# Gate products of a hybrid S5 / stick-breaking layer: 16 pairs of units by Strassen's scheme, and a later load of z

## Chip, cores and metric

One core of one Trainium2 chip runs the whole layer in one launch. The metric is device time in microseconds, lower is better. The engines are named as in the profile: PE (matmul), PEld (its weight load), DVE (vector), ACT (scalar), POOL, SP (issues most DMAs).

## Reference

```python
h = concat([meta, x])                       # 16 + 512 rows, D_MODEL = 2048
u, g_ssm, q, k, v, g_sb = split(h @ w_in)
y_ssm = (s5_branch(u, ...) * silu(g_ssm)) @ w_branch_ssm
y_sb  = (stick_breaking_attention(q, k, v) * silu(g_sb)) @ w_branch_sb
gates = sigmoid(h @ w_gate + b_gate)        # 2048 -> 4096
mixed = gates[:, :2048] * y_ssm + gates[:, 2048:] * y_sb
out   = layer_norm(ALPHA * h + mixed @ w_out)[16:]
```

Everything is float32. `s5_branch` ends in a GLU whose input is called z below.

## The kernel before

**Products.** Each float32 product is made of three fp32r matmuls: both operands are split into a rounded part (hi) and the rest (lo), and `mm3` (L131) adds hi·hi, hi·lo and lo·hi into the same PSUM tile. X is held split in SBUF (`Xh`, `Xl`: 16 chunks of 128 channels by 512 real columns and the meta columns).

**Weights.** All weights lie in `wst` as chunks of 128 x 1024 in the order of use. SP loads a chunk into one of three `raw` buffers (`load_upto`, L112); `prep_upto` (L119) makes `whi` with an ACT cast (L126) and `wlo` with a DVE subtraction (`split_lo`, printed as L96, as is every `tensor_tensor`). `whi` and `wlo` have three buffers each.

**Order.** The program is written out by hand. A `slot` (L164) is the work of one chunk: eight pieces, a piece being three matmuls, or more where it has several outputs. At its start a slot records the preparation of the chunk two slots ahead, and the finish of the unit that ended before; at its sixth piece it records the load of the chunk five ahead. ACT, DVE and SP each take their instructions in the recorded order. `schedule` hangs other work (`fillers`) onto piece numbers.

**Stages around the change.** First come the projections of each head with the SSM and the attention between them, in matmuls of 256 and 272 columns or of 512. Then eight units for g_ssm (`fin_gs`): a unit is 128 output channels, 16 pieces, 48 matmuls of 512 columns. In the last three of these units `load_z` (L1071) brings z back from DRAM in eight parts: SP loads a part into the only `zt` buffer, ACT casts it into `zh`, DVE subtracts into `zl`. Then the gates: 32 units of the same form, `fin_gate` (L1096) being a sigmoid with bias of 128 x 512 and a store. Then the GLU (`unit_act` on `zh`, `zl`; its first unit reads all eight parts of z in its eight pieces), the branch products with the mixing, the output product and the layer norm.

Of the kernel before, what the change touches and what calls it, by code (L numbers as in the profile page):

```python
# [38 lines left out]
def kernel(  # L39
# [20 lines left out]
    V, A, PE, SP, G = nc.vector, nc.scalar, nc.tensor, nc.sync, nc.gpsimd  # L60

    def pool(name, bufs=1, space=None, side=None):
        kw = dict(name=name, bufs=bufs)
        if space is not None:
            kw["space"] = space
        else:
            kw["reuse_waits"] = "tile"
            if side is not None:
                kw["side"] = side
        st = ExitStack()  # L70
        p = st.enter_context(tc.tile_pool(**kw))
        return p, st
# [9 lines left out]
    raw_p = ctx.enter_context(tc.tile_pool(name="raw", bufs=3))  # L82
# [24 lines left out]
    raws, his, los = {}, {}, {}  # L107
    issued = [0]
    prepped = [0]
    held = {}  # L110

    def load_upto(c):  # L112
        while issued[0] <= min(c, NCH - 1):
            t = raw_p.tile([P, 1024], F32, tag="raw", name="raw")
            SP.dma_start(out=t, in_=wst[use[issued[0]]])
            raws[issued[0]] = t
            issued[0] += 1

    def prep_upto(c):  # L119
        while prepped[0] <= min(c, NCH - 1):  # L120
# [10 lines left out]
    def mm3(o, ah, al, bh, bl, start, stop):  # L131
        PE.matmul(o, ah, bh, start=start, stop=False)  # L132
        PE.matmul(o, ah, bl, start=False, stop=False)  # L133
        PE.matmul(o, al, bh, start=False, stop=stop)  # L134
# [9 lines left out]
    gtd = [dram.tile([P, S], F32, name=f"gtd{i}") for i in range(2 * KT)]  # L144
# [19 lines left out]
    def slot(pieces, finish=None, chunks=1, ahead=2):  # L164
        c = ctr[0]
        prep_upto(c + chunks - 1 + ahead)
        while pend:
            pend.pop(0)()
        h = [his.pop(c + x) for x in range(chunks)]
        lo = [los.pop(c + x) for x in range(chunks)]  # L170
        if chunks == 1:
            h, lo = h[0], lo[0]
        for k, f in enumerate(pieces):
            if k == 5 and ahead:
                load_upto(c + chunks - 1 + ahead + 3)
            run_fillers()
            f(h, lo)
            piece[0] += 1
        ctr[0] += chunks
        if finish is not None:  # L180
            pend.append(finish)

    with tc.manual_schedule():

        xp, x_st = pool("x", side="left")
        Xh = xp.tile([P, KT, LP], F32R, name="Xh")
        Xl = xp.tile([P, KT, LP], F32R, name="Xl")
# [67 lines left out]
        bga = const.tile([P, 32], F32, name="bga")  # L255
# [318 lines left out]
        def store_pv():  # L574
            for src, dst in pvt_:
# [3 lines left out]
                                            in_=zer[:, None, :].to_broadcast([16, NG, 112]))  # L579
# [23 lines left out]
        def ta(nm, shape, dt_=F32, bufs=1):  # L603
            return ma.tile(shape, dt_, tag=nm, bufs=bufs, name=nm)
# [337 lines left out]
        def new_acc():  # L942
            return acc_p.tile([P, 512], F32, name="acc")
# [61 lines left out]
        for i in range(NT):  # L1005
# [47 lines left out]
            if i == 0:  # L1053
                mb_st, at = open_main()
# [6 lines left out]


        def fin_gs(a, j):
            t = zst["p"].tile([P, S], F32, tag="gsg", bufs=2, name="gsg") if zst else ta("us", [P, L])[:, 0:S]
            A.activation(t, a, ACTF.Sigmoid)
            tt(t, a, t, ALU.mult)
            A.dma_start(out=gd[j], in_=t)

        zst = {}

        def load_z(j):  # L1071
            if not zst:
                mb_st.close()
                ma_st.close()
                c_st.close()
                zst["so"], zst["so_st"] = pool("so", side="right")
                zst["p"], zst["st"] = pool("z", side="right")
                zst["h"] = zst["p"].tile([P, NT, S], F32R, name="zh")
                zst["l"] = zst["p"].tile([P, NT, S], F32R, name="zl")
# [6 lines left out]
        for j in range(NT):  # L1086
            unit_real(lambda a, j=j: fin_gs(a, j))
        run_fillers()
        assert not fillers
        zh, zl = zst["h"], zst["l"]  # L1090
        sh_ = zst["so"].tile([P, NT, S], F32R, name="sh")
        sl_ = zst["so"].tile([P, NT, S], F32R, name="sl")
        tmpl = lambda nm, b=1: zst["p"].tile([P, S], F32, tag=nm, bufs=b, name=nm)


        def fin_gate(a, j):  # L1096
            t = tmpl("gsg", 2)
            A.activation(t, a, ACTF.Sigmoid, bias=bga[:, j:j + 1])
            A.dma_start(out=gtd[j], in_=t)
# [6 lines left out]
        mp_, mhl_st = pool("mhl", side="left")  # L1106
        ctx.callback(mhl_st.close)
        mh = mp_.tile([P, KT, S], F32R, name="mh")
        ml = mp_.tile([P, KT, S], F32R, name="ml")
        ohp, oh_st = pool("oh", side="left")  # L1110
        oh_ = ohp.tile([P, NT, S], F32R, name="oh")
        ol_ = ohp.tile([P, NT, S], F32R, name="ol")
# [69 lines left out]
        pend.pop(0)()  # L1182
        ct_st.close()
        oh_st.close()
        zst["so_st"].close()
# [6 lines left out]
        for c in range(NCH - HOLD, NCH):  # L1192
# [4 lines left out]
        bias = fp.tile([P, D], F32, name="bias")  # L1197
# [73 lines left out]
        prep_upto(NCH - 1)  # L1271
# [114 lines left out]
```

## Time and profile before

| | |
|---|---|
| device time, three runs | 1471.38, 1472.03, 1474.52 us (median 1472.03) |
| profiled execution | 1473.17 us, its span 1471.4 us |
| PE busy | 1449.2 us, 7888 matmuls |
| DVE, ACT busy | 759.5 us, 409.9 us |
| mean granted TensorE clock | 0.995 |

The span runs from the first to the last instruction of the core. Matmuls overlap, so a matmul's own duration is longer than the distance from its start to the next one's; the distance is what it costs. The same holds in part for ACT and DVE, whose next instruction may start a little before the last one ends.

### The profile page before, as it was taken

To read this page: it belongs to the slowest core of one execution; us is meant where nothing else is said; L and a number is where in the kernel's file an instruction comes from. 1 tells how busy PE (TensorE), PEld (TensorE's weight loads), DVE (VectorE), ACT (ScalarE), POOL (GpSimd) and SP (SyncE) were. 2 spreads that over 40 slices of the span, in tenths; PEclk is the share of its full clock that TensorE was granted. 3 is DMA by queue.
4 is the path that set the end of the run, shared out by engine and by line. 5 is a ranking of instruction groups with operands and counts; after the bars stand their busy time and mean duration, and the time that the engine had idled before them with its cause. 6 is when DMAs were issued, how large, how long until landed. Compare 5 with 4: busy or idle time off the path is not lost.

```text
span 1471.4 us, 19233 instructions
## 1 busy us (share of the span) xinstructions
PE 1449.2 (98%) x7888; PEld 1257.1 (85%) x7888; DVE 759.5 (52%) x1145; ACT 409.9 (28%) x640; POOL 48.9 (3%) x95
## 2 busy tenths in 40 slices
PE   8999999999999999999999999999999999999996
PEld 7888999999999998888888888888888888888885
DVE  7987766666767667733222222222444444423357
ACT  5332323232323232323222222222332222221220
POOL 0840000000000000000000000000000000000000
PEclk9999999999999999999999999999999999999998
DMA  7354352525253434435333333333544444374223
GB/s 253 113 141 120 105 132 96 144 81 145 88 140 98 141 94 131 119 118 174 129 116 119 123 122 123 114 121 128 165 132 163 143 144 146 134 206 158 90 96 115
DMA packets 94040, 191.99 MB, mean 130 GB/s; under 512 B 28160, under 2 KB 41728, under 8 KB 93184
## 3 DMA queue, kind: packets, MB, share of 16 engines
q1 hardware_dynamic: 75248, 172.87, 38.8%
q10 hardware_dynamic: 18704, 17.90, 3.6%
q8 instruction: 62, 1.02, 0.3%
q14 instruction: 26, 0.21, 0.0%
HBM read 168.45 MB, written 22.28 MB: 130 GB/s over the span
## 4 chain that ended last, share of the span: by engine, by line
PE 95%; DVE 4%; DMA 0%; issue 0%; ACT 0%; SPq 0%; DVEq 0%; ACTq 0%
PE acc L132 27%; PE acc L133 27%; PE acc L134 27%; PE aux L132 3%; PE aux L134 2%; PE aux L133 2%; PE aux L771 1%; PE aux L732 1%; PE aux L767 1%; PE aux L878 1%; DVE Xl L96 1%; DVE wlo L96 1%; DMA xt<-xT 0%; PE aux L703 0%; PE aux L851 0%; PE aux L852 0%
## 5 line engine op out<-in xcount | busy, mean ns | idle before, releaser
L96 DVE TENSOR_TENSOR wlo<-raw,whi 128x1024 fp32r<-128x1024 f32 (+1 forms) x242 | 295.1, 1220 | 588.0 <-ACT whi L126 584.4
L132 PE MATMUL acc<-Xh,whi 128*128 128x512 f32 (+2 forms) x1664 | 576.4, 346 | 5.3 <-ACT whi L230 4.7
L133 PE MATMUL acc<-Xl,whi 128*128 128x512 f32 (+2 forms) x1664 | 570.3, 343 | 1.6 <-DVE Xl L96 1.2
L134 PE MATMUL acc<-Xh,wlo 128*128 128x512 f32 (+2 forms) x1664 | 569.1, 342 | 0.0
L126 ACT CAST whi<-raw 128x1024 fp32r<-128x1024 f32 x238 | 250.2, 1053 | 686.7 <-PE acc L133 570.1
L132 PEld LDWEIGHTS acc<-Xh,whi 128*128 128x128 f32 x1664 | 315.4, 190 | 40.7 <-ACT whi L230 4.7
L133 PEld LDWEIGHTS acc<-Xl,whi 128*128 128x128 f32 x1664 | 315.0, 189 | 36.5 <-DVE Xl L96 2.7
L134 PEld LDWEIGHTS acc<-Xh,wlo 128*128 128x128 f32 x1664 | 314.7, 189 | 35.5
L133 PE MATMUL acc<-sl,whi 128*128 128x512 f32 x128 | 49.8, 389 | 0.0
L134 PE MATMUL acc<-oh,wlo 128*128 128x512 f32 x128 | 49.8, 389 | 0.0
L132 PE MATMUL acc<-whi,mh 128*128 128x512 f32 x128 | 49.8, 389 | 0.0
L133 PE MATMUL acc<-wlo,mh 128*128 128x512 f32 x128 | 49.8, 389 | 0.0
L132 PE MATMUL acc<-zh,whi 128*128 128x512 f32 x128 | 49.8, 389 | 0.0
L133 PE MATMUL aux<-wlo,mh 128*128 128x512 f32 x128 | 49.8, 389 | 0.0
L134 PE MATMUL acc<-zh,wlo 128*128 128x512 f32 x128 | 49.8, 389 | 0.0
L132 PE MATMUL acc<-sh,whi 128*128 128x512 f32 x128 | 49.8, 389 | 0.0
L133 PE MATMUL acc<-ol,whi 128*128 128x512 f32 x128 | 49.8, 389 | 0.0
L132 PE MATMUL aux<-whi,mh 128*128 128x512 f32 x128 | 49.8, 389 | 0.0
L133 PE MATMUL acc<-zl,whi 128*128 128x512 f32 x128 | 49.8, 389 | 0.0
L134 PE MATMUL acc<-sh,wlo 128*128 128x512 f32 x128 | 49.8, 389 | 0.0
L132 PE MATMUL acc<-oh,whi 128*128 128x512 f32 x128 | 49.8, 389 | 0.0
L134 PE MATMUL aux<-whi,ml 128*128 128x512 f32 x128 | 49.8, 389 | 0.0
(233 smaller groups left out, 1474.2 us busy)
## 6 DMA issues: line engine op xcount, KB each, us to landing
raw<-wst SPq DMA_DIRECT2D x238, 512.0 KB
gtd<-gsg ACTq DMA_DIRECT2D x32, 256.0 KB
gt<-gtd SPq DMA_DIRECT2D x32, 256.0 KB
X<-brep SPq DMA_DIRECT2D x8, 512.0 KB
X<-pvd SPq DMA_DIRECT2D x16, 256.0 KB
X<-sd SPq DMA_DIRECT2D x8, 512.0 KB
xs<-xr SPq DMA_DIRECT2D x8, 512.0 KB
xt<-xT SPq DMA_DIRECT2D x7, 528.0 KB
```

Of the source, the lines that this page charges most:

```text
L96: eng.tensor_tensor(out, a, b, op)
L126: A.copy(h, t)
L132: PE.matmul(o, ah, bh, start=start, stop=False)
L133: PE.matmul(o, ah, bl, start=False, stop=False)
L134: PE.matmul(o, al, bh, start=False, stop=stop)
L732: PE.matmul(vp[:, g, 0:NK], W["vt"][:, g].rearrange("p r q -> p (r q)"), ut[:, g * NK:g * NK + NK], start=True, stop=True,)
L767: PE.matmul(yp[:, g, 0:SK], W["ot"][:, g].rearrange("p t c -> p (t c)"), hs[:, g * NK + MK - 1:g * NK + MK - 1 + SK], start=True, stop=False,)
L771: PE.matmul(yp[:, g, 0:SK], W["mt"][:, g, :], ut[:, g * NK + MK:g * NK + MK + SK], start=False, stop=True,)
L878: PE.transpose(o, W["A"][:, k0:k0 + kn], ident)
```

## The change

The 32 gate units become 16 pairs. A pair is one 256-channel-wide block of the two gate halves (output channels j and 16+j), with X halved in two ways: by input channels (chunks 0 to 7 and 8 to 15) and by columns (0 to 255 and 256 to 511). Strassen's scheme (in Winograd's form) makes the four output quarters out of seven products instead of eight; each product is a slot of 24 matmuls of 256 columns. For that:

- `factor` makes four sums of weight chunks per pair on DVE, each 128 x 1024 (`s1`, `s2`, and two in place), so that the seven factors that are cast and split come from four loaded chunks. The fourth chunk has buffers of its own (`r22`).
- `sums_b` makes sums of X on DVE during the last g_ssm units, from X loaded a second time (`load_b`, 16 DMAs), splits three of them into `T1`, `T2`, `T3`, and leaves the fourth for `split_t4` in the first pair. These tiles take the place in SBUF that z had.
- `e0` to `e6` put the quarters together: one copy by ACT, five DVE sums of 256 columns, four sigmoids of 256 columns and two stores per pair. With `soon` they are recorded ahead of the preparation in a slot.
- z gets its tiles when the last pair has done with T1 to T3, and is loaded in that pair's last three slots (`open_z`, `load_z` every third piece). `zt` still has one buffer.
- The pools of the GLU and mixing stages change sides.

```diff
+    def factor(w, x):
+        if x == 0:
+            return w["11"]
+        if x == 1:
+            w["s1"] = sev["p"].tile([P, 1024], F32, tag="s1", name="s1")
+            w["s2"] = sev["p"].tile([P, 1024], F32, tag="s2", name="s2")
+            tt(w["s1"], w["21"], w["22"], ALU.add)
+            tt(w["s2"], w["s1"], w["11"], ALU.subtract)
+            return w["s2"]
+        if x == 2:
+            return w["s1"]
+        if x == 3:
+            tt(w["21"], w["11"], w["21"], ALU.subtract)
+            return w["21"]
+        if x == 4:
+            return w["12"]
+        if x == 5:
+            tt(w["s2"], w["12"], w["s2"], ALU.subtract)
+            return w["s2"]
+        return w["22"]
...
-            t = raws.pop(i)
+            pr = pair_of(i)
+            t = raws.pop(i) if pr is None else factor(sev[pr[0]], pr[1])
...
-    def slot(pieces, finish=None, chunks=1, ahead=2):
+    def slot(pieces, finish=None, chunks=1, ahead=2, soon=False):
         c = ctr[0]
+        while pend and soon:
+            pend.pop(0)()
         prep_upto(c + chunks - 1 + ahead)
...
+        def load_b(c):
+            t = sevst["xp"].tile([P, 2, L], F32, tag="xb", bufs=2, name="xb")
+            for e in range(2):
+                SP.dma_start(out=t[:, e, :], in_=xT[:, c + 8 * e, :])
...
+        def sums_b(c):
...
+            tt(b11, b12, b11, ALU.subtract)
+            tt(b12, b22, b12, ALU.subtract)
+            A.copy(row("1h"), b11)
+            tt(b22, b22, b11, ALU.subtract)
+            A.copy(row("3h"), b12)
+            tt(jk(sevst["t4"][:, c, :], SK), b21, b22, ALU.subtract)
+            A.copy(row("2h"), b22)
+            for x, b_ in (("1", b11), ("3", b12), ("2", b22)):
+                split_lo(row(x + "l"), b_, row(x + "h"))
+        schedule([(80, open_sev), (80, lambda: load_b(0)), (81, lambda: load_b(1))]
+                 + [(86 + 5 * c, lambda c=c: sums_b(c)) for c in range(8)]
+                 + [(87 + 5 * c, lambda c=c: load_b(c + 2)) for c in range(6)])
...
-        schedule([(80 + 6 * j, lambda j=j: load_z(j)) for j in range(NT)])
...
+        def pair(j):
+            tw = lambda nm, n=256: sev["p"].tile([P, n], F32, tag=nm, bufs=2, name=nm)
+            a, b, c = (new_acc()[:, 0:256] for _ in range(3))
+            ops = [
+                (a, Xh[:, 0:8, 0:256], Xl[:, 0:8, 0:256], True),
+                (b, sevst["2h"], sevst["2l"], True),
+                (c, sevst["1h"], sevst["1l"], True),
+                (b, sevst["3h"], sevst["3l"], False),
+                (a, Xh[:, 8:16, 0:256], Xl[:, 8:16, 0:256], False),
+                (c, Xh[:, 8:16, 256:512], Xl[:, 8:16, 256:512], False),
+                (b, t4h, t4l, False),
+            ]
...
+            def e3():
+                W[1] = tw("gb", S)
+                t = tw("u3")
+                tt(t, b, W["p1"], ALU.add)
+                tt(t, t, c, ALU.add)
+                sig(1, 1, t)
...
+            def e5():
+                tt(W["u2"], W["u2"], c, ALU.add)
+                sig(0, 1, W["u2"])
+                A.dma_start(out=gtd[j], in_=W[0])
+            def e6():
+                tt(W["p1"], W["p1"], b, ALU.add)
+                sig(1, 0, W["p1"])
+                A.dma_start(out=gtd[KT + j], in_=W[1])
...
+                if j == KT - 1 and x == 4:
+                    schedule([(0, open_z)] + [(1 + 3 * k, lambda k=k: load_z(k)) for k in range(NT)])
+                slot([mk(kk) for kk in range(8)], (e0, e1, None, e3, e4, e5, e6)[x], soon=True)
+        schedule([(4 + 6 * k, lambda k=k: split_t4(2 * k)) for k in range(4)])
+        for j in range(KT):
+            pair(j)
...
-        for j in range(KT):
-            unit_real(lambda a, j=j: fin_gate(a, j))
-            unit_real(lambda a, j=j: fin_gate(a, KT + j))
```

The order of the instructions at three places follows. In the changed kernel `raw` is a loaded chunk, `s_` a sum of chunks, `u_` and `p_` the sums of quarters.

DVE in the gates, before: one row, the split of each chunk.

```order
L96 TENSOR_TENSOR wlo<-raw,whi 128x1024 x65
```

DVE in one pair of the change, from the sum of `e5` of the pair before on:

```order
L96 TENSOR_TENSOR u_7316<-u_7316,acc 128x256
L96 TENSOR_TENSOR s_7449<-raw 128x1024
L96 TENSOR_TENSOR s_7450<-s_7449,raw 128x1024
L96 TENSOR_TENSOR wlo<-s_7450,whi 128x1024
L96 TENSOR_TENSOR p_7285<-p_7285,acc 128x256
L96 TENSOR_TENSOR wlo<-s_7449,whi 128x1024
L96 TENSOR_TENSOR raw<-raw 128x1024
L96 TENSOR_TENSOR wlo<-raw,whi 128x1024
...
L96 TENSOR_TENSOR s_7450<-raw,s_7450 128x1024
L96 TENSOR_TENSOR wlo<-s_7450,whi 128x1024
L96 TENSOR_TENSOR u_7614<-acc,p_7515 128x256
L96 TENSOR_TENSOR u_7614<-u_7614,acc 128x256
```

The sums of chunks and of quarters now stand between the splits.

ACT in the gates, before: two casts, then the finish of a unit.

```order
L126 CAST whi<-raw 128x1024 x2
L1098 ACTIVATE gsg<-acc,bga 128x512
L1099 DMA gtd_132<-gsg 128x512
L126 CAST whi<-raw 128x1024 x2
L1098 ACTIVATE gsg<-acc,bga 128x512
```

ACT in one pair of the change:

```order
L1198 ACTIVATE ga<-u_9846,bga 128x256
L1223 DMA gtd_126<-ga 128x512
L171 CAST whi<-s_9980 128x1024
L1198 ACTIVATE gb<-p_9815,bga 128x256
L1228 DMA gtd_142<-gb 128x512
L171 CAST whi<-s_9979 128x1024
L1203 COPY p_10045<-acc 128x256
L171 CAST whi<-raw 128x1024 x2
L171 CAST whi<-s_9980 128x1024
```

Of the seven casts of a pair three now read a sum of chunks (`s_`) and one reads a chunk that DVE changed in place; sigmoids that read `u_` or `p_` stand between the casts.

ACT where z is loaded (`zt`, `zh`), before, during the g_ssm units:

```order
L1082 CAST zh<-zt 128x512 x2
L126 CAST whi<-raw 128x1024
L1082 CAST zh<-zt 128x512
L126 CAST whi<-raw 128x1024
L1065 ACTIVATE gsg<-acc 128x512
```

ACT where z is loaded in the change, in the last three slots of the last pair:

```order
L1198 ACTIVATE gb<-u_10600,bga 128x256
L171 CAST whi<-raw 128x1024
L1180 CAST zh<-zt 128x512 x3
L1198 ACTIVATE ga<-acc,bga 128x256
L171 CAST whi<-raw 128x1024
L1180 CAST zh<-zt 128x512 x2
L1198 ACTIVATE ga<-u_10536,bga 128x256
L1223 DMA gtd_129<-ga 128x512
L171 CAST whi<-raw 128x1024
L1180 CAST zh<-zt 128x512 x3
```

The three casts of weights among these rows belong to the last factor of the gates and to the first two chunks of the GLU.

## Rows read from the trace of the kernel before

**Rows 1.** The page's first part: busy time, share of the span, instructions of each engine.

```profile
PE 1449.2 (98%) x7888; PEld 1257.1 (85%) x7888; DVE 759.5 (52%) x1145; ACT 409.9 (28%) x640; POOL 48.9 (3%) x95
```

**Rows 2.** The page's chain that ended last, by engine.

```profile
PE 95%; DVE 4%; DMA 0%; issue 0%; ACT 0%; SPq 0%; DVEq 0%; ACTq 0%
```

**Rows 3.** Waits of PE, longest in total first: engine, line, releaser: us, times, longest.

```profile
PE acc L132 <- ACT whi L230: 4.7, 1, 4.7
PE aux L732 <- DVE X L96: 1.7, 1, 1.7
```

**Rows 4.** Windows: stretch, length, busy us (count) by engine, clock, DMA share, GB/s.

```profile
675.55:1023.71 348.16, 348.16 (x1537) 288.29 (x1536) 81.63 (x68) 88.12 (x99) 0.00 (x0) 1.00 0.38 126
```

**Rows 5.** Timeline of PE in a key projection: start, us, instruction.

```profile
243.84 0.28 PE L132 MATMUL acc<-Xh,whi 128*128 128x256 f32 x1
244.19 0.29 PE L132 MATMUL acc<-Xh,whi 128*128 128x272 f32 x1
...
246.77 0.28 PE L132 MATMUL acc<-Xh,whi 128*128 128x256 f32 x1
```

**Rows 6.** DVE by line and shape: count, busy us, mean ns, idle before.

```profile
L96 DVE TENSOR_TENSOR wlo<-raw,whi 128x1024 fp32r<-128x1024 f32 x238 | 292.3, 1229 | 587.1 <-ACT whi L126 584.4 <-PE aux L852 1.6 <-PE acc L134 0.8
...
L96 DVE TENSOR_TENSOR ot<-ot,X 128x1024 f32<-128x1024 f32 x8 | 9.8, 1222 | 0.2
...
L96 DVE TENSOR_TENSOR gsig<-aux,gs 128x256 f32<-128x256 f32 x16 | 6.6, 412 | 1.7 <-PE aux L134 1.7
...
L96 DVE TENSOR_TENSOR zl<-zt,zh 128x512 fp32r<-128x512 f32 x8 | 5.5, 693 | 21.5 <-ACT zh L1082 21.5
```

**Rows 7.** Timeline of DVE, three wide instructions that follow each other.

```profile
600.37 1.22 DVE L96 TENSOR_TENSOR X<-cb,be 128x1024 f32<-128x1024 f32 x1
601.63 1.23 DVE L96 TENSOR_TENSOR ot<-ot,X 128x1024 f32<-128x1024 f32 x1
602.77 1.22 DVE L96 TENSOR_TENSOR wlo<-raw,whi 128x1024 fp32r<-128x1024 f32 x1
```

**Rows 8.** ACT by line and shape.

```profile
L126 ACT CAST whi<-raw 128x1024 fp32r<-128x1024 f32 x238 | 250.2, 1053 | 686.7 <-PE acc L133 570.1 <-PE acc L134 57.0 <-PE aux L134 30.7
L1098 ACT ACTIVATE gsg<-acc,bga 128x512 f32<-128x512 f32 x32 | 21.8, 682 | 4.6 <-PE acc L134 4.6
...
L855 ACT ACTIVATE sg<-aux 128x264 f32<-128x264 f32 x16 | 6.3, 394 | 25.4 <-DVE Aall L96 22.0 <-DVE Aall L864 3.4
```

**Rows 9.** Timeline of ACT at the end of the gates.

```profile
1023.91 0.69 ACT L1098 ACTIVATE gsg<-acc,bga 128x512 f32<-128x512 f32 x1 [4.61 <-PE acc L134]
1024.63 0.33 ACTq L1099 DMA_DIRECT2D gtd<-gsg  x1
1025.05 1.05 ACT L126 CAST whi<-raw 128x1024 fp32r<-128x1024 f32 x1 [0.45 <-ACT gsg L1098]
```

**Rows 10.** Timeline of SP, ACT and DVE: the load of z, its first part and its end.

```profile
648.02 0.33 SPq L1081 DMA_DIRECT2D zt<-zd  x1
...
650.74 0.62 ACT L1082 CAST zh<-zt 128x512 fp32r<-128x512 f32 x1 [6.27 <-DMA zt<-zd]
...
652.11 4.36 SPq L1081 DMA_DIRECT2D zt<-zd  x2
...
680.81 0.69 DVE L96 TENSOR_TENSOR zl<-zt,zh 128x512 fp32r<-128x512 f32 x1 [2.16 <-ACT zh L1082]
```

**Rows 11.** Windows at an early stretch with gaps on PE (columns as in Rows 4).

```profile
102.00:106.00 4.00, 2.75 (x25) 2.53 (x24) 4.00 (x5) 0.62 (x1) 0.00 (x0) 1.00 0.23 59
112.00:115.00 3.00, 1.34 (x11) 1.12 (x11) 2.55 (x4) 0.00 (x0) 0.00 (x0) 1.00 0.00 0
116.00:120.00 4.00, 4.00 (x23) 4.00 (x23) 2.95 (x5) 2.71 (x6) 0.00 (x0) 0.57 0.10 20
```

**Rows 12.** A window at the start of the kernel, the highest rate of the DMAs.

```profile
8.00:12.00 4.00, 3.77 (x13) 3.06 (x13) 3.30 (x6) 3.03 (x6) 0.00 (x0) 1.00 1.04 396
```

More of the change, by code (lines that the diff above doesn't have):

```diff
@@ L110, with load_raw, load_upto, prep_upto @@
     held = {}
[L112 to L116, printed above, removed]
-            issued[0] += 1
-    def prep_upto(c):
-        while prepped[0] <= min(c, NCH - 1):
+    GATES = 96
+    NSEV = KT
+    NFAC = NCH + 3 * NSEV
+    pair_of = lambda f: divmod(f - GATES, 7) if GATES <= f < GATES + 7 * NSEV else None
+    chunk_of = lambda f: f if f < GATES else f - 3 * NSEV
+    sev = {}
+    def load_raw(c, p_=None, tag="raw", **kw):
+        t = (p_ or raw_p).tile([P, 1024], F32, tag=tag, name="raw", **kw)
+        SP.dma_start(out=t, in_=wst[use[c]])
+        return t
+    def load_upto(f):
+        while issued[0] <= min(f, NFAC - 1):
+            i = issued[0]
+            pr = pair_of(i)
+            if pr is None:
+                raws[i] = load_raw(chunk_of(i))
+            else:
+                c = GATES + 4 * pr[0]
+                w = sev.setdefault(pr[0], {})
+                if pr[1] == 0:
+                    w["11"], w["21"] = load_raw(c), load_raw(c + 2)
+                    w["22"] = load_raw(c + 3, sev["p"], "r22", bufs=2)
+                elif pr[1] == 1:
+                    w["12"] = load_raw(c + 1)
+            issued[0] += 1
+    def factor(w, x):
[18 more added lines that the diff above has]
+        return w["22"]
+    def prep_upto(f):
+        while prepped[0] <= min(f, NFAC - 1):
             i = prepped[0]
-            t = raws.pop(i)
+            pr = pair_of(i)
+            t = raws.pop(i) if pr is None else factor(sev[pr[0]], pr[1])
             hp, lp = held.get(i, (hi_p, lo_p))
@@ L129, in prep_upto, with mm3 @@
             prepped[0] += 1
[L131 to L134, printed above, removed]
+    def mm3(o, ah, al, bh, bl, start, stop, **kw):
+        PE.matmul(o, ah, bh, start=start, stop=False, **kw)
+        PE.matmul(o, ah, bl, start=False, stop=False, **kw)
+        PE.matmul(o, al, bh, start=False, stop=stop, **kw)
     jk = lambda ap, n: ap.rearrange("p (j k) -> p j k", k=n)
@@ L1063, in fin_gs @@
         def fin_gs(a, j):
-            t = zst["p"].tile([P, S], F32, tag="gsg", bufs=2, name="gsg") if zst else ta("us", [P, L])[:, 0:S]
+            t = sev["p"].tile([P, S], F32, tag="ga", bufs=2, name="gsg") if sev else ta("us", [P, L])[:, 0:S]
             A.activation(t, a, ACTF.Sigmoid)
@@ L1069, with open_sev @@
         zst = {}
-        def load_z(j):
[L1072 to L1079, printed above, removed]
+        sevst = {}
+        def open_sev():
+            mb_st.close()
+            ma_st.close()
+            c_st.close()
+            sev["p"], sevst["w"] = pool("sev", side="right")
+            sevst["t4"] = sev["p"].tile([P, 8, 256], F32, name="t4r")
+            sevst["tp"], sevst["t"] = pool("sevt", side="right")
+            for x in "123":
+                for nm in "hl":
+                    sevst[x + nm] = sevst["tp"].tile([P, 8, 256], F32R, name=f"T{x}{nm}")
+            sevst["xp"], sevst["x"] = pool("sevx", side="right")
@@ new lines @@
+        schedule([(80, open_sev), (80, lambda: load_b(0)), (81, lambda: load_b(1))]
+                 + [(86 + 5 * c, lambda c=c: sums_b(c)) for c in range(8)]
+                 + [(87 + 5 * c, lambda c=c: load_b(c + 2)) for c in range(6)])
+        for j in range(NT):
+            unit_real(lambda a, j=j: fin_gs(a, j))
+        run_fillers()
+        assert not fillers
+        sevst["x"].close()
+        tmpl = lambda nm, b=1: zst["p"].tile([P, S], F32, tag=nm, bufs=b, name=nm)
+        t4h, t4l = Xh[:, 0:8, 256:512], Xl[:, 0:8, 256:512]
@@ L1080, in load_z, with split_t4, open_z @@
+        def split_t4(c):
+            cs_ = slice(c, c + 2)
+            A.copy(t4h[:, cs_, :], sevst["t4"][:, cs_, :])
+            split_lo(t4l[:, cs_, :], sevst["t4"][:, cs_, :], t4h[:, cs_, :])
+        def open_z():
+            sevst["t"].close()
+            zst["p"], zst["st"] = pool("z", side="right")
+            zst["h"] = zst["p"].tile([P, NT, S], F32R, name="zh")
+            zst["l"] = zst["p"].tile([P, NT, S], F32R, name="zl")
+        def load_z(j):
             t = zst["p"].tile([P, S], F32, tag="zt", bufs=1, name="zt")
@@ L1083, in load_z, with sig, e0, e1 @@
             split_lo(zst["l"][:, j, :], t, zst["h"][:, j, :])
-        schedule([(80 + 6 * j, lambda j=j: load_z(j)) for j in range(NT)])
-        for j in range(NT):
-            unit_real(lambda a, j=j: fin_gs(a, j))
+        def pair(j):
+            tw = lambda nm, n=256: sev["p"].tile([P, n], F32, tag=nm, bufs=2, name=nm)
+            a, b, c = (new_acc()[:, 0:256] for _ in range(3))
+            W = {}
+            ops = [
[7 more added lines that the diff above has]
+            ]
+            def sig(u, half, src):
+                A.activation(W[u][:, 256 * half:256 * half + 256], src, ACTF.Sigmoid,
+                             bias=bga[:, KT * u + j:KT * u + j + 1])
+            def e0():
+                W["p1"] = tw("p1")
+                A.copy(W["p1"], a)
+            def e1():
+                W["u2"] = tw("u2")
+                tt(W["u2"], b, W["p1"], ALU.add)
+            def e3():
[4 more added lines that the diff above has]
+                sig(1, 1, t)
+            def e4():
+                W[0] = tw("ga", S)
+                sig(0, 0, a)
+            def e5():
[6 more added lines that the diff above has]
+                A.dma_start(out=gtd[KT + j], in_=W[1])
+            for x, (o, bh, bl, first_) in enumerate(ops):
+                def mk(kk, o=o, bh=bh, bl=bl, first_=first_, x=x):
+                    def f(h, lo):
+                        ws = slice(kk * P, (kk + 1) * P)
+                        mm3(o, h[:, ws], lo[:, ws], bh[:, kk, :], bl[:, kk, :], first_ and kk == 0, kk == 7,
+                            skip_group_check=True)
+                    return f
+                if j == KT - 1 and x == 4:
+                    schedule([(0, open_z)] + [(1 + 3 * k, lambda k=k: load_z(k)) for k in range(NT)])
+                slot([mk(kk) for kk in range(8)], (e0, e1, None, e3, e4, e5, e6)[x], soon=True)
@@ L1090 @@
         zh, zl = zst["h"], zst["l"]
[L1091 to L1099, printed above, removed]
-        for j in range(KT):
-            unit_real(lambda a, j=j: fin_gate(a, j))
-            unit_real(lambda a, j=j: fin_gate(a, KT + j))
         pend.pop(0)()
         x_st.close()
[L1106 to L1109, printed above, removed]
+        sop, so_st = pool("so", side="left")
+        sh_ = sop.tile([P, NT, S], F32R, name="sh")
+        sl_ = sop.tile([P, NT, S], F32R, name="sl")
         ohp, oh_st = pool("oh", side="left")
@@ L1152 @@
         zst["st"].close()
+        sevst["w"].close()
+        mp_, mhl_st = pool("mhl", side="right")
+        ctx.callback(mhl_st.close)
+        mh = mp_.tile([P, KT, S], F32R, name="mh")
+        ml = mp_.tile([P, KT, S], F32R, name="ml")
         ctp, ct_st = pool("ct", side="right")
@@ L1184 @@
         oh_st.close()
-        zst["so_st"].close()
+        so_st.close()
         fp, f_st = pool("fin", side="left")
@@ L1191 @@
         ctx.callback(wl_st.close)
-        for c in range(NCH - HOLD, NCH):
+        for c in range(NFAC - HOLD, NFAC):
             held[c] = (wlp, wlp)
@@ L1270 @@
         c = ctr[0]
-        prep_upto(NCH - 1)
+        prep_upto(NFAC - 1)
         while pend:
```

4 lines of the change are left out of this document (added).

## Prediction

> **What bounds the kernel now.** Read the busy times first [rows 1]: PE works 1449.2 of 1471.4 us, and the chain that ended last lies on PE for 95% [rows 2]. PE hardly waits: its two longest waits are 4.7 us at the start and 1.7 us in the first head [rows 3]. So a microsecond less on PE is a microsecond less in all, as long as the others keep up, and a wait of PE costs its length.
>
> Then take the gates alone. From their first matmul to the first of the GLU pass 348.16 us, all of it PE work at a granted clock of 1.00 [rows 4]. That is 32 units of 48 matmuls, 1536 matmuls of 512 columns, one every 348.16 / 1536 = 0.2267 us. DVE is busy there for 81.6 us and ACT for 88.1 us: both have a lot of room, and that is what the change spends.
>
> **PE's share of the gates.** Removed: 1536 matmuls of 512 columns. Added: 16 pairs x 7 products x 8 chunks x 3 = 2688 matmuls of 256 columns. What one costs is in the key projection, where triples of 256 and of 272 columns alternate, each matmul with its own weights as in the pairs: four rounds of 3 + 3 take 246.77 - 243.84 = 2.93 us [rows 5], 0.122 us a matmul; the triple of 256 alone takes 0.35 us (244.19 - 243.84), 0.117 us each. At the other end, a matmul of 512 pays 0.2267 - 512 / 2400 = 0.0134 us beyond its columns at 2.4 GHz (the gates' clock is 1.00 of it); with the same on 256 it would be 0.120 us. I take 0.119. A slot is then 24 x 0.119 = 2.86 us, a pair 20.0 us (19.7 to 20.2), all pairs 320 us. If PE alone counted, the gates would win 28 us (26 to 33).
>
> **DVE and ACT in a pair.** Neither is full: DVE has per pair 7 splits and 4 sums of 128 x 1024, each 1.22 us [rows 6], and 5 sums of 256 columns at 0.41 us, together 15.5 us; ACT has 7 casts of 1.05 us and five small operations [rows 8], some 10 us. Both are under 20.0 us. But they work in turns. A split needs its cast, a cast of a sum needs the sum, and both engines take their instructions in the order recorded (the listing of the change above). Before, DVE's waits for the cast cost nothing: 584 us of them stand in one row [rows 6], because a slot lasted 5.4 us. Now it lasts 2.86 us. I follow the queues through one pair, from the sum of `e5` on, with distances from start to start: on DVE 1.14 us for a wide instruction if the next needs nothing of it (602.77 - 601.63), 1.25 us if it does (601.63 - 600.37) [rows 7], 0.33 or 0.45 us for a narrow one (0.41 less 0.09 or plus 0.04); on ACT 1.09 us from a cast's start to its split's.
>
> - DVE's own: 7 splits x 1.14 = 8.0; 4 wide sums x 1.25 = 5.0; narrow sums 2 x 0.33 + 3 x 0.45 = 2.0. Sum 15.0 us.
> - ACT's time in which DVE can do nothing: the casts of factors 1, 3 and 5, which need the sum just made, 3 x 1.09; the cast of factor 2, which stands in ACT's queue behind the sigmoid of `e6` (it needs the narrow sum) and a store, 0.55 + 0.42 + 1.09; the cast of factor 6 behind the sigmoid of `e3`, 0.42 + 1.09; some 0.2 for factor 0. Sum 7.0 us. The casts of factors 0 and 4 are otherwise hidden.
>
> The 0.42 of a store is the distance from its issue to the cast behind it (1025.05 - 1024.63) [rows 9]. A sigmoid of 256 columns with bias is not in the trace; it lies between 0.394 us (264 columns, no bias) and 0.682 us (512 columns, with bias) [rows 8], and I take 0.51, near the middle.
>
> So the two engines need **22.0 us per pair** and PE only 20.0: PE waits 2 us in each pair, at its factors 1 to 3, whose preparation is the longest. Bounds: 21.3 if each step is 3% shorter, 23.0 if no instruction starts before the one ahead has ended. Fifteen pairs take 330 us.
>
> **Start.** Each `sums_b` is four narrow sums and three narrow splits, about 2.8 us of DVE every five pieces (15 x 0.2267 = 3.4 us), with a wide split per slot and the g_ssm products beside it: for eight chunks 22.4 + 5 x 1.14 + 2 x 0.68 = 29.5 us of work in 27.2 us. DVE comes into the gates 2 to 3 us behind, and ahead of two factors that need wide sums. `split_t4` puts 4 x 0.69 = 2.8 us more on DVE in the first pair. Two slots of prepared weights cover part of this; I take 22 + 2.8 + 1.2 = 26 us for that pair. The queue of SP is new too: 16 loads of 264 KB and about 9 weight chunks of 512 KB in some 32 us, 280 GB/s, where the gates move 126 [rows 4] and the start of the kernel 396 [rows 12]. That fits; if it does not, the pair takes up to 33 us, and with no loss at all 22.
>
> Gates together: 26 + 330 = 356 us, **7.8 us more than before**.
>
> **z.** Before, the eight loads of z ran beside the g_ssm units and PE did not wait. One part takes a chain: issue 648.02, cast 650.74, split, next issue 652.11, 4.1 us, since there is one `zt` buffer; from the first issue to the end of the eighth split 681.50 - 648.02 = 33.5 us [rows 10]. The change moves the chain, as slow as it is, to the last three slots of the gates: its first load can start when PE begins slot 4 of the last pair, 0.3 us in, so the last part is ready at 33.8 and the last piece of the first GLU slot ends at 34.5. PE has meanwhile 3 x 2.86 + 5.44 = 14.0 us of work. It waits **20.5 us** (19.5 to 24, as ACT and DVE have other work between the parts and weight loads stand between them in SP's queue). Recording the parts every third piece changes nothing: the issue waits for the buffer. The casts of the first two GLU chunks stand in ACT's queue behind the third and the fifth part, at 13 and 21 us, so PE stops first for weights, then for z. Behind this SP holds the next weights, but those of the third chunk are on their way before; nothing more is late after the first GLU slot.
>
> **Clock.** 1.25 us of PE idle in 4 us left the clock at 1.00; after a stretch with 1.34 us of work in 3 us it stood at 0.57 for the four us from 116 to 120 [rows 11], which lost 4 x 0.43 = 1.7 us. The waits of a pair are 2 us spread over some 9 us, so I count none for them, and one fall after the wait for z: **1.7 us**. The Trainium skill, "TensorE: Matmul & The Clock Gate", section "HAM oscillation — how this bites in real kernels", describes a kernel whose matmuls stop for data in every tile and whose clock falls to half in every tile. Carried over, each of the 16 pairs would have a fall; by the rows that is the second rival below, by the row of 102 to 106 it is none.
>
> **Sum.** 1473.2 (the profiled execution, 1.1 above the median 1472.0) + 7.8 + 20.5 + 1.7 = 1503.2; against the median 1502. I say **1503 us**, slower by 31.
>
> **Rivals.**
> - *PE binds the pairs after all, so the change wins.* If the turns of DVE and ACT came under 20.0 us a pair, the gates would take 320 us: -28.2 + 20.5 + 1.7 = -6, 1466 us. The point at which it decides: the gates have to gain 22.2 us to pay for z, which leaves 326 us, 20.1 us a pair with the start's extra. For it: the busy sums, 15.5 and 10 us. Against: the queues' order, and that 22.0 would need to be 8% shorter while its long terms are rows with hundreds of instructions. Chance 0.09.
> - *The clock falls in every pair.* PE loses up to 1.7 us a pair and, if that falls on slots 4 to 6, `e5` comes later and the whole turn with it: 16 x 1.7 = 27 us more, 1530. For it: short waits in each pair; against: the first row of [rows 11], a longer wait without a fall. Chance 0.08.
> - *z is hidden as before.* 1481 to 1483 us. It would need loads ahead of the buffer; nothing in the program does that. Chance 0.05.
>
> **Numbers.** My forecast has 0.78. Its own bounds: low 16 x 21.3 + 2 = 343 for the gates (-5), z 19.5, no fall: 1487; high 33 + 15 x 22.7 = 373 (+25), z 24, 2 x 1.7: 1525. The range is 1482 to 1526: it takes in the third rival and leaves out the first two, 0.17. A change within 0.2% (2.9 us) could not be told from none. Slower by more: 0.89; faster by more: 0.08, the first rival; within: 0.03, between the two.
>
> **What would show it.** Right: gates of about 356 us with PE busy some 320 of it; pairs 22 us apart; PE's waits led by the split and cast of weights (2 us a pair) and by `zl` (some 20 us once); DVE waiting for casts about 7 us a pair, while its busy share in the gates is only 70%. Wrong: pairs 20.0 us apart with no waits on PE (first rival), a clock under 0.95 over the pairs (second), or a first GLU slot of 5.4 us (third).

## The result, and the profile after

The changed kernel takes **1508.4 us** (median of four runs, 1506.3 to 1509.8) against 1472.3 us for the kernel before on the same chip: a ratio of 1.024 (95% interval 1.022 to 1.026), 36 us slower. Forecast were 1503 us, with a range of 1482 to 1526. The profiled execution took 1507.9 us, its span is 1506.1.

The page's busy times and its chain by engine, after:

```profile
PE 1440.1 (96%) x9040; PEld 1295.2 (86%) x9040; DVE 942.0 (63%) x1397; ACT 482.0 (32%) x764; POOL 48.8 (3%) x95
...
PE 67%; DVE 17%; ACT 8%; issue 5%; DMA 2%; ACTq 0%; SPq 0%; DVEq 0%
```

PE works 9 us less than before, and the span is 35 us longer [rows 1]: PE now waits. The chain, 95% PE before [rows 2], runs through DVE and ACT for a quarter of the span, though DVE is busy only 63% of it.

**The pairs.** PE's timeline after, the first matmuls of three pairs (`T2h` is the operand of product 1) and two waits in the pair before them:

```profile
710.61 0.39 PE L179 MATMUL acc<-T1h,wlo 128*128 128x256 f32 x1 [0.45 <-DVE wlo L96]
714.52 0.35 PE L177 MATMUL acc<-T3h,whi 128*128 128x256 f32 x1 [1.01 <-DVE u L96]
...
728.98 0.28 PE L177 MATMUL acc<-T2h,whi 128*128 128x256 f32 x1
...
751.02 0.28 PE L177 MATMUL acc<-T2h,whi 128*128 128x256 f32 x1
...
773.06 0.28 PE L177 MATMUL acc<-T2h,whi 128*128 128x256 f32 x1
```

A pair takes 22.04 us. In each, PE waits for the split of a sum, and for `e1`, which must have read the PSUM tile that the T3 product goes on to write. The two waits make some 1.4 us, and a pair is 1.9 us longer than PE alone needs (20.16 us, measured below): a matmul's recorded time is 0.16 us longer than what it costs (0.28 against 0.12), so that much of a wait does not show as idle, and the first matmul behind a wait is slower. Windows after (columns as in [rows 4]): thirteen of the pairs, and the first GLU slot, from the last gate matmul to the first matmul of the second slot:

```profile
728.98:1018.00 289.02, 270.82 (x2206) 265.75 (x2205) 193.66 (x210) 120.95 (x159) 0.00 (x0) 1.00 0.34 120
1034.85:1061.12 26.27, 12.54 (x26) 6.70 (x25) 7.87 (x11) 7.39 (x12) 0.00 (x0) 0.64 0.36 118
```

Over the pairs DVE is busy 193.7 of 289.0 us (67%), and the clock is at 1.00. The gates run from 673.44 to 1034.85, 361.4 us against 348.2 before [rows 4]: sixteen times 22.04 makes 352.6, so the start costs 8.8.

**The start.** DVE's timeline after, while it makes the sums of X, and PE's two longest waits in the first pair:

```profile
648.18 0.43 DVE L96 TENSOR_TENSOR t4r<-xb 128x256 f32<-128x256 f32 x1 [3.19 <-DMA gd<-us]
664.92 0.43 DVE L96 TENSOR_TENSOR xb<-xb 128x256 f32<-128x256 f32 x1 [3.04 <-DMA xb<-xT]
```

```profile
678.82 0.39 PE L177 MATMUL acc<-T2h,whi 128*128 128x256 f32 x1 [2.35 <-ACT whi L171]
...
691.27 0.35 PE L177 MATMUL acc<-T3h,whi 128*128 128x256 f32 x1 [2.26 <-DVE u L96]
```

DVE stood still for two transfers. The first is a store, issued by ACT, that still read the place of the fourth sum's tile. The second is a load of X. SP could issue it only at 658.01, when DVE had done with the chunk two before it (`xb` has two buffers); three weight chunks had gone just ahead of it, and the DMA engines were nearly full until it landed:

```profile
654.35 1.38 SPq L123 DMA_DIRECT2D raw<-wst  x3
658.01 1.04 SPq L1136 DMA_DIRECT2D xb<-xT  x2
```

```profile
658.00:665.00 7.00, 7.00 (x32) 5.80 (x31) 3.86 (x9) 2.17 (x4) 0.00 (x0) 1.00 0.98 350
679.00:685.00 6.00, 4.88 (x25) 4.46 (x26) 4.42 (x10) 2.97 (x6) 0.00 (x0) 0.72 0.11 44
```

The second window is in the first pair: the clock falls there. From 680.38 to 683.59 us fifteen matmuls stand 0.214 us apart in place of 0.120, 1.4 us more.

**z.** ACT's timeline after (the second, third and last cast of z), then PE's around the end of the first GLU slot:

```profile
1034.55 0.62 ACT L1180 CAST zh<-zt 128x512 fp32r<-128x512 f32 x1 [3.95 <-DMA zt<-zd]
1038.60 0.62 ACT L1180 CAST zh<-zt 128x512 fp32r<-128x512 f32 x1 [3.44 <-DMA zt<-zd]
...
1058.71 0.62 ACT L1180 CAST zh<-zt 128x512 fp32r<-128x512 f32 x1 [3.41 <-DMA zt<-zd]
```

```profile
1040.58 0.80 PE L177 MATMUL acc<-zh,whi 128*128 128x512 f32 x1 [5.57 <-ACT whi L171]
...
1059.38 0.80 PE L177 MATMUL acc<-zh,whi 128*128 128x512 f32 x1 [2.08 <-ACT zh L1180]
...
1061.12 0.63 PE L177 MATMUL acc<-zh,whi 128*128 128x512 f32 x1
1061.55 0.63 PE L178 MATMUL acc<-zl,whi 128*128 128x512 f32 x1
...
1066.09 0.40 PE L177 MATMUL acc<-zh,whi 128*128 128x512 f32 x1
```

A part every 4.05 us. The first GLU slot lasts 26.3 us in place of 5.4: a wait of 20.8. Behind it eleven matmuls stand 0.427 us apart in place of 0.227 (the clock at its lower level), 2.2 us more. Inside the slot the clock is at that level twice, up to 1045.4 and again from 1051.3 on; that time is part of the 20.8.

Gates +13.2, z +20.8, clock +2.2, and the gates begin 2.1 us earlier than before (673.44 against 675.55): 34.1 of the 34.7 us between the two spans. (Over the runs of this record the gates begin between 673.3 and 676.8 us, so the 2.1 may be chance.)

### The profile page after: what moved, and what is told of

Its sections match the earlier page's. It is cut to its first block, busy times and chain, and to the rows that moved or that the text cites. A ratio compares the mean times of both kernels' runs of the same rounds, so it can differ in the third digit from the quotient of the medians.

```text
span 1506.1 us, 22031 instructions
## 1 busy us (share of the span) xinstructions
PE 1440.1 (96%) x9040; PEld 1295.2 (86%) x9040; DVE 942.0 (63%) x1397; ACT 482.0 (32%) x764; POOL 48.8 (3%) x95
## 4 chain that ended last, share of the span: by engine, by line
PE 67%; DVE 17%; ACT 8%; issue 5%; DMA 2%; ACTq 0%; SPq 0%; DVEq 0%
PE acc L177 18%; PE acc L178 18%; PE acc L179 18%; ACT whi L171 6%; DVE wlo L96 5%; DVE s L96 4%; PE aux L177 3%; PE aux L179 2%; PE aux L178 2%; DVE u L96 2%; DVE raw L96 1%; DMA zt<-zd 1%; PE aux L818 1%; PE aux L779 1%; PE aux L814 1%
## 5 line engine op out<-in xcount | busy, mean ns | idle before, releaser
L177 PE MATMUL acc<-Xh,whi 128*128 128x256 f32 (+2 forms) x1664 | 520.9, 313 | 6.7 <-ACT whi L277 4.6
L178 PE MATMUL acc<-Xl,whi 128*128 128x256 f32 (+2 forms) x1664 | 515.0, 309 | 2.3 <-DVE Xl L96 2.2
L179 PE MATMUL acc<-Xh,wlo 128*128 128x256 f32 (+2 forms) x1664 | 514.0, 309 | 0.0
L96 DVE TENSOR_TENSOR wlo<-s,whi 128x1024 fp32r<-128x1024 f32 x48 | 58.8, 1225 | 69.8 <-ACT whi L171 69.8
L171 ACT CAST whi<-s 128x1024 fp32r<-128x1024 f32 x48 | 50.3, 1048 | 89.0 <-DVE s L96 81.5
L177 PE MATMUL acc<-zh,whi 128*128 128x512 f32 x128 | 53.2, 416 | 13.4 <-ACT zh L1180 7.8
L177 PE MATMUL acc<-T3h,whi 128*128 128x256 f32 x128 | 37.4, 292 | 17.4 <-DVE u L96 17.4
L178 PE MATMUL acc<-zl,whi 128*128 128x512 f32 x128 | 52.9, 413 | 0.3 <-DVE zl L96 0.2
```

The lines of the kernel that those rows point to most:

```text
L177: PE.matmul(o, ah, bh, start=start, stop=False, **kw)
L178: PE.matmul(o, ah, bl, start=False, stop=False, **kw)
L179: PE.matmul(o, al, bh, start=False, stop=stop, **kw)
```

## Experiments

Three causes are to be told apart: what sets the pair, what holds z, what the start costs. The runs were made on several chips; the kernel before takes 1472.1 to 1472.6 us on them, so medians are compared as they stand.

### What sets the pair

**The order within the preparation.** The next factor's sum is recorded between a cast and its split, and the finish of the slot before stands there too, behind the cast in place of ahead of it:

```diff
             A.copy(h, t)
+            while mid:
+                mid.pop(0)()
+            q = pair_of(i + 1)
+            if q is not None:
+                nxt[i + 1] = factor(sev[q[0]], q[1])
             split_lo(lo, t, h)
```

> The changed kernel with the same instructions in another order in each slot of the gates: the cast first, then the finish of the slot before, then DVE's sum for the next factor, then the split. The sum of factor f+1 so runs while ACT casts factor f, and no cast stands behind a sigmoid of the same slot. Theory (turns): DVE's 15 us and ACT's 10 us run beside each other, PE becomes the bound: pairs 20.0 to 20.2 us apart, 16 x 1.9 = 30 us less, about 1478 us (1473 to 1484), the wait for z unchanged at some 21 us. Rival (the engines' throughput or PE's own pace at 256 columns holds the pairs at 22.0): 1505 to 1510 us.

Measured: **1474.4 us** (ten runs, ratio 1.0015, interval 1.0006 to 1.0024), 34.0 us under the changed kernel with the same instructions, 30 of them in the sixteen pairs. DVE's timeline of one pair, first after, then reordered:

```profile
728.93 0.41 DVE L96 TENSOR_TENSOR p<-p,acc 128x256 f32<-128x256 f32 x1
731.37 1.23 DVE L96 TENSOR_TENSOR wlo<-s,whi 128x1024 fp32r<-128x1024 f32 x1 [2.02 <-ACT whi L171]
732.51 1.22 DVE L96 TENSOR_TENSOR raw<-raw 128x1024 f32<-128x1024 f32 x1
734.84 1.23 DVE L96 TENSOR_TENSOR wlo<-raw,whi 128x1024 fp32r<-128x1024 f32 x1 [1.11 <-ACT whi L171]
735.99 0.42 DVE L96 TENSOR_TENSOR u<-acc,p 128x256 f32<-128x256 f32 x1
...
739.87 1.23 DVE L96 TENSOR_TENSOR wlo<-s,whi 128x1024 fp32r<-128x1024 f32 x1 [1.20 <-ACT whi L171]
...
743.40 2.53 DVE L96 TENSOR_TENSOR wlo<-raw,whi 128x1024 fp32r<-128x1024 f32 x2 [1.52 <-ACT whi L171]
...
749.83 1.23 DVE L96 TENSOR_TENSOR wlo<-s,whi 128x1024 fp32r<-128x1024 f32 x1 [1.17 <-ACT whi L171]
```

```profile
741.32 0.42 DVE L96 TENSOR_TENSOR p<-p,acc 128x256 f32<-128x256 f32 x1 [0.65 <-PE acc L186]
741.65 1.22 DVE L96 TENSOR_TENSOR raw<-raw 128x1024 f32<-128x1024 f32 x1
742.79 1.22 DVE L96 TENSOR_TENSOR wlo<-s,whi 128x1024 fp32r<-128x1024 f32 x1
745.16 1.22 DVE L96 TENSOR_TENSOR wlo<-raw,whi 128x1024 fp32r<-128x1024 f32 x1 [1.15 <-ACT whi L173]
```

In the changed kernel DVE waits for casts 2.02 + 1.11 + 1.20 + 1.52 + 1.17 = 7.02 us in a pair, nearly all its idle time there. In the new order the wait of 2.02 us is gone: DVE makes the next sum (`raw<-raw`) while ACT casts. Two pair starts of the reordered kernel, three pairs apart, and a window of it:

```profile
703.68 0.28 PE L184 MATMUL acc<-T2h,whi 128*128 128x256 f32 x1
...
764.16 0.28 PE L184 MATMUL acc<-T2h,whi 128*128 128x256 f32 x1
```

```profile
740.00:980.00 240.00, 240.00 (x2002) 240.00 (x2001) 179.27 (x191) 109.66 (x142) 0.00 (x0) 1.00 0.40 132
```

60.48 / 3 = 20.16 us a pair, PE without a gap. The order set the pair, not the amount of work. The edit moves the next sum and the finish together; what each of the two brings is not told apart.

**The finish behind the preparation.** The other way round: `soon=True` becomes `soon=False` in the pairs.

> Edit: in the changed kernel the finish of a slot stands behind the preparation of the slot two ahead, instead of in front of it. Theory (DVE and ACT take turns, and the place of the finish in their queues sets the pair): a walk through the two queues with the durations of the trace gives 22.6 us per pair in place of 22.04, so about 9 us more over 16 pairs, a span near 1515 us, and first T2h matmuls 22.6 apart. Rival (the order within a slot does not matter, only the sum of DVE's work and of the ACT passes it waits for): the pairs stay 22.0 apart and the span within 2 us of 1506.

Measured: 1533.6 us (one run), 25 us slower than the changed kernel; the theory's sign, but nearly three times its size. Four of PE's waits, in two pairs:

```profile
715.61 0.35 PE L177 MATMUL acc<-T3h,whi 128*128 128x256 f32 x1 [1.92 <-DVE u L96]
...
721.91 0.36 PE L177 MATMUL acc<-Xh,whi 128*128 128x256 f32 x1 [0.33 <-DVE u L96]
...
738.46 0.36 PE L177 MATMUL acc<-T3h,whi 128*128 128x256 f32 x1 [1.91 <-DVE u L96]
...
746.26 0.36 PE L177 MATMUL acc<-Xh,whi 128*128 128x256 f32 x1 [0.33 <-DVE u L96]
```

```profile
736.00:738.40 2.40, 0.54 (x5) 0.34 (x3) 2.40 (x4) 0.72 (x1) 0.00 (x0) 1.00 0.87 236
738.40:742.00 3.60, 3.54 (x18) 3.58 (x19) 2.27 (x2) 1.04 (x1) 0.00 (x0) 0.57 0.91 354
```

The wait for `e1` is 1.9 us in place of 1.0. From it to the next wait it is 6.30 us in the first of these pairs and 7.80 in the second, where the clock stands at 0.57. So a pair is 22.85 us, near the 22.6 of the theory, and 24.35 where the clock falls, which it does behind 10 of the 15 such waits from 715 us on: 15 x 0.8 + 10 x 1.5 = 27 us (waits for z that are 1.6 us shorter take back a part). A fall costs 1.5 us here, near the 1.7 of the prediction's second rival: what that rival foresaw is one re-ordering away. The Trainium skill, "TensorE: Matmul & The Clock Gate", section "HAM oscillation — how this bites in real kernels", tells of a kernel that waits for data at every tile, longer than PE waits in these pairs, and whose clock falls at every tile. These traces show falls behind waits of 1.9 us in two of three pairs, and none behind waits of 1.0 us (changed kernel, 1.00 over 289 us) or of 1.6 us (the next run, 1.00 over 290 us).

**A lead of three slots.** A fourth buffer for `whi` and `wlo`, `ahead=3`; for room, most small tiles of the pairs have one buffer:

> The changed kernel with factors prepared three slots ahead in place of two: every fourth factor has a fourth pair of hi and lo buffers; to make room, the small tiles p1, u2, u3 and gb have one buffer. Theory (ACT and DVE taking turns need 22.0 us a pair, whatever the lead): pairs 21.9 to 22.0 us apart, the start of the gates up to 3 us shorter, total 1504 to 1509 us. Rival (the lead of two short slots is too little, the engines have room): pairs 20.0 us apart, about 1476 us.

Measured: 1506.2 us (one run); first matmuls of pairs at 817.00 and 904.88, four pairs apart: 21.97 us. More lead doesn't help: each pair brings the two queues 22 us of turns, and a lead is used up once. The Trainium skill, "Perfetto Trace Analysis", section "Optimization Strategy", says that the same gap repeating on the engine that should be full can mean too few buffers. In these runs the repeating gap went with the order and not with one more buffer. The single buffers of the small tiles may hide a part of a gain: PE waits 1.6 us a pair for `e1` in this kernel in place of 1.0.

### What holds z

**Four z buffers.** `bufs=1` of `zt` becomes 4, nothing else.

> The changed kernel with four zt buffers in place of one; nothing else. Theory (one buffer makes the eight loads of z a chain of 4.1 us each): four loads are under way at once, then a part costs the longer of its cast and its split, 0.7 us; all eight are ready some 9 us after slot 4 of the last pair begins, when PE has just ended the pairs. The wait of PE at the first GLU slot falls from 20.8 us to 1 to 4 us, the clock does not fall after it (2.2 us): about 1488 us (1485 to 1493). Pairs stay 22.0 us apart. Rival (PE waits there for the GLU's weights, which SP loads late, or for DMA bandwidth): gain under 5 us, 1503 or more.

Measured: 1499.8 us (ratio 1.0192, 1.0175 to 1.0209): a gain of 8.7 us, between the two expectations and met by neither. SP's queue in this kernel:

```profile
1026.36 0.81 SPq L1179 DMA_DIRECT2D zt<-zd  x2
1027.36 0.34 SPq L123 DMA_DIRECT2D raw<-wst  x1
1027.73 0.91 SPq L1179 DMA_DIRECT2D zt<-zd  x2
1036.97 0.33 SPq L123 DMA_DIRECT2D raw<-wst  x1
1037.35 1.37 SPq L1179 DMA_DIRECT2D zt<-zd  x3
```

The fifth z load stands behind a weight load, and that one waits until 1036.97 for a `raw` buffer. The buffer comes free when DVE has split it (1035.72 to 1036.95); the cast of that split stands in ACT's queue behind the third cast of z, which waited for its load until 1033.76. Three engines wait for each other in a ring, some 9 us a round (the next weight load goes at 1046.20, behind the next split).

**Staged z loads.** The loads are taken out of that ring: parts 0 to 3 go into the tile of the fourth sum, idle since the first pair, during the last pair's first product; parts 4 to 7 go into four `zt` buffers at once.

```diff
+                if j == KT - 1 and x == 0:
+                    schedule([(2 * k, lambda k=k: fetch_z(k)) for k in range(4)])
                 if j == KT - 1 and x == 4:
-                    schedule([(0, open_z)] + [(1 + 3 * k, lambda k=k: load_z(k)) for k in range(NT)])
+                    schedule([(0, open_z)] + [(0, lambda k=k: fetch_z(k)) for k in range(4, NT)]
+                             + [(1 + 3 * k, lambda k=k: load_z(k)) for k in range(NT)])
```

> Edit: in the changed kernel, nothing but the staged z loads (chunks 0 to 3 in the tile of the fourth sum during the last pair's first product, chunks 4 to 7 in four z buffers at once). Changed kernel 1508.4 us, with four z buffers alone 1499.8; the first GLU slot waits 20.8 us there and the clock costs 2.2. Theory (z waits for its loads): what is left is the z work of DVE and ACT, eight casts and splits of 0.6 us, on engines that have no room in a pair of 22.04 us, so 5 to 8 us of wait and one fall of the clock: 1494 (1490 to 1497). Rival (without the reordering the full turns of DVE and ACT hold z as much as the loads did): 1498 or more.

Measured: **1485.8 us** (ratio 1.0086, 1.0069 to 1.0103), 22.6 us under the changed kernel, of the 23.0 that z and its clock cost. What PE still waits for z, by the list of its waits from 1000 us on:

```profile
PE acc L178 <- DVE zl L96: 0.8, 1, 0.8
```

Better than the theory's 5 to 8 us. It took the engines as full; but behind the last pair come plain chunks, and DVE's last wide sum lies before the z work, so both engines have room in just these slots: DVE's last wide sum starts at 1027.36 us, its first split of z at 1034.43, and until 1047 us it still waits 2.08 us for each of two casts of weights.

**Both, with the new order.** First the reordered kernel with four z buffers:

> Both edits: the new order in the gates' slots and four zt buffers. Theory: the two costs are separate and add: 1508 - 30 - 20 = 1458 us (1451 to 1464), 14 us less than the kernel before the change. Rival (with pairs of 20 us the loads of weights or z collide, or the clock falls): over 1466 us.

Measured: 1465.2 us (ratio 0.9952, 0.9937 to 0.9966), faster than before, but at the edge between theory and rival: the first GLU slot still takes 15 us, since SP's ring is the same (the fifth load of z stands behind a weight load that goes at 1005.84, 8 us after the loads ahead of it). Then with staged loads:

> Edit: on top of the reordered preparation with four z buffers; chunks 0 to 3 of z are loaded into the tile of the fourth sum (8 KB per partition, idle since the first pair) during the last pair's first product, chunks 4 to 7 into the four z buffers at once, so that no z load stands behind a weight load that waits. Reordered kernel with four z buffers: 1465.2 us, in whose stretch 995 to 1020 us PE is idle for 6.3 us and at half clock for about 2 us more. Theory (SP's queue held the z loads): the three DMA waits of ACT's z casts, 3.6, 4.5 and 3.4 us, go; what is left is the work itself, eight casts and eight splits of 0.6 us each on engines that have about 0.7 us free per slot, so a PE idle of 2 to 3 us in place of 6.3: about 1460 us (1457 to 1463). Rival (the turns of the two engines hold z, not its loads): PE idle stays 5 us or more and the time at or above 1464.

Measured: **1452.8 us** (ratio 0.9868, 0.9854 to 0.9881), below the expected band: the list of PE's waits from 690 to 1100 us is empty. The two causes add: 34.0 alone and 22.6 alone make 56.6; together they bring 55.6.

### What the start costs

The opening of the space, the loads of X and the eight sums, four pieces earlier (80, 81, 86 and 87 in their table become 76, 77, 82 and 83). In the changed kernel:

> Edit: in the changed kernel, nothing but the opening of the space, the loads of X and the eight sums of X four pieces (2.7 us) earlier. Changed kernel: 1508.4 us; its gates take 361.4 us, of which 16 pairs of 22.04 us are 352.6, so the start loses 8.8. Theory (the sums of X come late into DVE's queue and push the first factors back): the start loses 2 to 4 us less, 1505.5 (1504 to 1506.5). Rival (the first pair is long because of the same turns as the other pairs and of the splits of the fourth sum): within 1.5 us of 1508.4.

Measured: 1505.3 us (1504.7 to 1509.2; ratio 1.0227, 1.0211 to 1.0243). The interval overlaps that of the changed kernel: unsettled. In the traces the gates are 1.7 us shorter, less than the theory's 2 to 4. On the reordered kernel with four z buffers:

> Edit: on top of the reordered preparation with four z buffers; opening of the space, loads of X and the eight sums of X all four pieces (2.7 us) earlier. In that kernel PE is idle 4.5 us between 675 and 690 us, behind DVE, which is busy 14.35 of those 15 us. Theory (the sums end late because they begin late): PE's idle there falls by 2 to 2.7 us: 1462.7 (1461 to 1464). Rival (a wait of the sums for the store of the SSM input, at 648 us, and for the X loads, at 665 and 669 us, holds them wherever they stand): no gain, 1464 to 1466.

Measured: 1459.3 us (ratio 0.9911, 0.9898 to 0.9925), 5.9 less than without and below the expected band. By the traces PE's waits between 675 and 690 us fall from 4.4 to 1.8 us, as expected, and its waits for z by 1.5. The two profiled executions differ by 3.4 us and the medians by 5.9, so the gain's size is less sure than its sign. Of DVE's waits for transfers the one for the store is gone; one of 3.3 us for a load of X stays.

### All together

The new order, the staged z, the earlier start, and T3 in a pool of its own, so that the space of T1 and T2 is free for `zh` and `zl` one slot earlier:

> Edit: the reordered preparation, the staged z loads, the sums of X four pieces earlier, and the space of T1 and T2 freed for zh and zl one slot earlier (T3 in a pool of its own), so that the eight casts of z spread over four slots in place of three. Theory (the three causes, order within the preparation, z's loads, the start, add up): 1465.2, less 5 for the loads, less 2.5 for the start, less 2 for the slot more that z has: 1455.7 (1453 to 1459), 16 us under the kernel before. Rival (they share a cause, the length of DVE's queue): not under 1460.

Measured: **1449.1 us** (five runs, 1447.8 to 1451.5; ratio 0.9846, 0.9832 to 0.9859), 23 us faster than the kernel before and 59 faster than the change, and below the expected band: the staged loads, counted at 5 us, had already brought 12.4 (1465.2 against 1452.8). Its page, and below it the last of these rows in the page of the changed kernel:

```profile
PE 1423.1 (98%) x9040; PEld 1290.3 (89%) x9040; DVE 942.7 (65%) x1397; ACT 483.2 (33%) x764; POOL 49.4 (3%) x95
...
PE 92%; DVE 5%; DMA 1%; issue 1%; ACT 0%; SPq 0%; DVEq 0%; ACTq 0%
...
L96 DVE TENSOR_TENSOR wlo<-s,whi 128x1024 fp32r<-128x1024 f32 x48 | 58.7, 1223 | 24.3 <-ACT whi L173 24.3
```

```profile
L96 DVE TENSOR_TENSOR wlo<-s,whi 128x1024 fp32r<-128x1024 f32 x48 | 58.8, 1225 | 69.8 <-ACT whi L171 69.8
```

DVE and ACT are as busy as in the changed kernel; DVE's wait ahead of the splits of sums is 24.3 us where it was 69.8. PE is the bound again, and the gates take 325.3 us (674.39 to 999.64) for 348.2 before. The scheme pays nearly what PE alone promised, 22.9 of 25.6 us; the changed kernel had lost it in queues. PE has no wait between 690 and 1100 us, but neither has it with the staged loads alone (1452.8 us), so nothing here shows that the pool of T3 adds to the gain.

## Why the prediction was right, step by step

- **PE's share.** 0.119 us a matmul was forecast, 20.0 us a pair, 28 us to win. PE alone takes 20.16 a pair (0.120), 25.6 us to win over sixteen. Shown by the reordered kernel. The pair lies within its bounds (19.7 to 20.2), the win just under its own (26 to 33): by those bounds of the pair, 348.2 less 16 x 20.2 leaves 25.0, so its lower end was put 1 us too high.
- **Turns of DVE and ACT.** Forecast 22.0 us a pair, measured 22.04; the new order and the lead of three slots show that it is the turns. It was not luck: DVE's wait for casts, forecast at 7.0 us a pair, is 7.02. One reading was wrong: PE's waits were to be led by the split and cast of weights, and the longer one is for the sum of `e1` (1.0 us, against 0.4 for a split). That a product can wait for its PSUM tile was left out. The pair's length came out even so, since that sum stands in DVE's queue right behind the split of factor 3 (735.99 in the rows above) and comes late by the same turns. The guessed sigmoid of 256 columns (0.51 us) took 0.510 from a sum and 0.466 from PSUM.
- **Start.** The mis-sized term: 4 us forecast over a pair of 22, 8.8 measured. It is as large as the miss of the whole sum (1507.9 us against 1503.2, for the profiled execution). Of the missing 4.8 the fall of the clock in the first pair is 1.4; the prediction had no term for it. It had none either for the store, for which DVE, late already, stood still 3.2 us. "That fits", said of SP's queue and its loads, failed for one load, for which DVE stood still 3.0 us: a mean of 280 GB/s was compared with 396 in a fast stretch [rows 12] (the fastest, 12 to 16 us, has 413), while the load could go only when its buffer was free and the DMA engines moved 350 at a share of 0.98. That these 6.2 us hold the rest of the missing 4.8 is argued; shown is only that an earlier start, in which the wait for the store is gone, brings time back with the new order.
- **z.** 20.5 us forecast from one buffer and a chain of 4.1 us a part; 20.8 measured, 4.05 us a part. Staging brings back 22.6 with the clock. But the rule behind it, that the issue waits for the buffer, was half of it: it held with one buffer, and with buffers enough the queue held the loads.
- **Clock.** One fall forecast behind the wait for z, at 1.7 us; it costs 2.2. None was forecast in the pairs: so it is from the second pair on, but the first has one.
- **The rivals.** *PE binds the pairs* needed 20.1 us a pair to break even with z as it is; the reordered kernel has 20.16 and comes out 2 us slower than before. Its condition was right, and false only for the order as written. *The clock falls in every pair* did not occur, but came in two of three pairs once the wait was 1.9 us. *z hidden* did not occur: nothing in the program did it.

## What to carry to other kernels

Two half-busy engines that hand each tile on to each other can bind a kernel: add their turns in queue order, not their busy times, and record an instruction that depends on nothing new between the two halves of a hand-over. When a load comes late though buffers are free, look at what stands ahead of it in its queue and for whom that waits. Before giving up a scheme that saves work on the busiest engine, find out whether the loss is in the scheme or in the order.

## What the hardware showed beyond this

- A wait of 1.0 us (with one of 0.4) per 22 us left the clock at 1.00, and so did one of 1.6 us (the lead of three slots); one of 1.9 us (with one of 0.3) was followed by the lower level in 10 of 15 pairs. A single wait of 2.26 us, in the first pair of the changed kernel, was followed by 1.00 (691 to 697 us), so the length of one wait does not settle it.
- The lower clock costs a short matmul less than its ratio of two: in the pairs with a fall, 256 columns go from 0.120 to 0.213 us, a factor of 1.78, and behind the wait for z 512 columns go from 0.227 to 0.427, 1.88. At the lower level both are their columns at 1.2 GHz; at the upper one each carries 0.013 us beyond them.
